# Layer 2's first seven products made from the un-normed residual, and normed as they leave

## The chip, the core and the metric

The kernel runs on one core of one Trainium2 chip. The metric is the device time of one execution in microseconds (us). Times are read from one profiled execution of the kernel before; the changed kernel is known here only as code and as the order of its instructions.

## What is computed

One inference step of a 2-layer decoder trunk for 320 tokens (256 of a prompt, 8 x 8 of samples), 2048 channels, float32. Cut to what matters here:

```python
def layer_norm(x, g, b):
    mu = jnp.mean(xf, -1, keepdims=True)
    var = jnp.mean(jnp.square(xf - mu), -1, keepdims=True)
    return (xf - mu) * lax.rsqrt(var + LN_EPS) * g + b
...
def mixer_layer(x, ...):
    h = x @ w_in
    ...
    y = merged @ w_out
    x_new = layer_norm(alpha * x + y, ln_g, ln_b)
...
    for l in range(DEPTH):
        xp, ... = mixer_layer(xp, ...)
        xs, ... = mixer_layer(xs, ...)
```

So layer 2's input projection `x @ w_in` needs layer 1's norm, which needs the whole residual `alpha * x + y` of a token.

## The kernel before

Activations lie transposed: 128 channels on the partitions, the 320 tokens in the row. A vector of 2048 channels is 16 tiles of 128x320, four to a buffer (`[128, 4, T]`, T = 320). Weights come in blocks of 128x128, eight to a chunk of 128x1024. Everything is held as a high and a low part in float32r (`hl`, `split_h`, `split_l`): ACT copies the high part, DVE (or POOL) subtracts it for the low part. A block then costs three matmuls into one PSUM tile: high weight x high tile, low x high, high x low (`block`, `block_low`).

`run` walks through a fixed list of jobs (`layer_groups`), a job being one 128-row strip of a product, with 16 blocks for most. Layer 2 begins with a group of four jobs that share each tile (kc 0, vc 0, qc 0, qc 1: attention's keys, values and queries), 16 x 12 products; then qc 2, qc 3, kc 1 and vc 1 alone, 48 products each. Eight blocks make a chunk: the first group is eight chunks, a single job two. Chunk c + 2's high split is issued at the start of chunk c, its low split in the middle; a low split goes to POOL when the kernel's own count of DVE's work is high. The PSUM tiles of such jobs are three (`pd`), and a job that ends is read out by its `done_` function.

All engines take their instructions in the order in which the program issues them (`manual_schedule`), so the order of the Python code sets the work. Background work (attention, retention) is stepped by `pump` once a chunk.

At the end of a layer `done_wo` adds each strip of the out-projection to the residual in `z` and sums it and its square over the tiles in `S` and `Q`. After strip 15, PE sums both over the partitions (`token_sums`, 6 small matmuls), DVE and ACT make mean and reciprocal deviation of each token, and PE spreads them over the partitions (`token_rows`, 2 x 3 matmuls). `norm` then centres (tiles 1 to 15 on POOL), scales (DVE), applies scale and offset and copies the high part (ACT) and subtracts for the low part (DVE). Its generator `rest` is written two to three tiles deep, and `need_x(k + 3)` steps it ahead of each tile of the first group:

```python
            for k in range(16):
                if k < 12:
                    center(k + 4, nc.gpsimd)
                if k < 13:
                    scaled(k + 3)
                if k < 14:
                    high(k + 2)
                if k:
                    low(k)
                yield
```

Lines of helpers in the profile: L196 is `mm`, L205 `tr`, L175 `act` (copies too), L182 `tt`, L186 `stt`, L191 `ts`.

Of the kernel before, what the change touches and what calls it, by code (L numbers as in the profile page):

```python
# [17 lines left out]
D = 2048  # L18
DEPTH = 2
NP = 256  # L20
NB, NT = 8, 8
T = NP + NB * NT
PAST = 1024
HA, DK, DV = 4, 128, 256
# [16 lines left out]
def att_rows(t):  # L41

    p, g = divmod(t, 4)
    lo, hi = (2 * p) * 4 + g, (2 * p + 1) * 4 + g
    return np.concatenate([np.arange(lo * 64, lo * 64 + 64), np.arange(hi * 64, hi * 64 + 64)])


# [43 lines left out]
class Job:  # L91
    __slots__ = ("kind", "i", "ps", "left", "w")

    def __init__(self, kind, i):
        self.kind, self.i, self.ps, self.left = kind, i, None, n_k(kind)


class Step:
# [200 lines left out]
    def setup(self):  # L299
        nc, io = self.nc, self.io  # L300
        self.ident = self.const("ident", [128, 128])
        make_identity(nc, self.ident[:])
        self.ident_r = self.cp.tile([128, 128], F32R, tag="ident_r", name="ident_r")
        nc.vector.tensor_copy(out=self.ident_r, in_=self.ident)
        self.ones = self.const("ones", [128, 128])
        nc.vector.memset(self.ones, 1.0)
        self.ones_r = self.cp.tile([128, 128], F32R, tag="ones_r", name="ones_r")
        nc.vector.memset(self.ones_r[:].bitcast(F32), 1.0)
        yield
# [15 lines left out]
        self.pscale = self.const("pscale", [128, DEPTH, 8], io["pool_scale"])  # L325
        self.lng = self.const("lng", [128, DEPTH, 16], io["ln_g"])
        self.lnb = self.const("lnb", [128, DEPTH, 16], io["ln_b"])
        self.bmask = self.const("bmask", [128, 4, 80], io["c_bmask"])
# [5 lines left out]
    def run(self):  # L334
# [30 lines left out]
        for layer in range(DEPTH):  # L365
            if layer:
                self.begin_layer(layer)
            for grp in layer_groups():
                jobs = [Job(kind, i) for kind, i in grp]
                self.before(jobs[0].kind, jobs[0].i)  # L370
                for k in range(n_k(grp[0][0])):
                    if len(jobs) > 1:
                        self.need_x(min(k + 3, 15))
                    for n, job in enumerate(jobs):
                        if pos == 0:
                            self.split_h(c + 2)
                        if pos == CH // 2:
                            self.split_l(c + 2)
                            self.load(c + 6)
                        self.block(job, k, c, pos)  # L380
                        pos += 1
# [11 lines left out]
    def block(self, job, k, c, pos):  # L393
        if job.ps is None:
            if job.kind == "qc" and job.i == 1:
                job.ps = self.p([128, T])
            else:
                job.ps = self.pd.tile([128, T], F32, tag="d", name="d")
# [14 lines left out]
    def part(self, pair, k):  # L413
        return pair[0][k // 4][:, k % 4, :], pair[1][k // 4][:, k % 4, :]

# [17 lines left out]
    def begin_layer(self, l):  # L433
        self.l, zs = l, getattr(self, "z", None)
        self.gated, self.pt, self.acc, self.sig = {}, {}, None, {}
        self.xk = 0
        self.x_gen = self.x_from_input() if l == 0 else self.norm(l - 1, zs, False)
        self.oC = [None, None]
# [5 lines left out]
    def need_x(self, k):  # L444
        while self.xk <= k:
# [4 lines left out]
            self.xk += 1  # L450

    def x_from_input(self):
        self.x = ([], [])
        for k in range(16):
            if k % 4 == 0:
                self.x[0].append(self.g([128, 4, T], F32R, name=f"xh{k}"))
                self.x[1].append(self.g([128, 4, T], F32R, name=f"xl{k}"))
            h, lo = self.part(self.x, k)
# [3 lines left out]
    def before(self, kind, i):  # L462
# [11 lines left out]
        if kind == "wo" and i == 0:  # L474
            self.z = [self.g([128, 4, T], name=f"z{n}") for n in range(4)]


# [243 lines left out]


    def done_kc(self, p, ps):
        nc, l = self.nc, self.l
        kv = self.g([128, 2, T], name="kv")
        self.copy(kv[:, 0, :], ps)
        nc.gpsimd.dma_start(out=self.io["o_wk"][l, p], in_=kv[:, 0, 128:T])
# [6 lines left out]
    def done_vc(self, p, ps):  # L734
        nc, l = self.nc, self.l
        kv = self.att[p]["kv"]
        self.copy(kv[:, 1, :], ps)
        nc.gpsimd.dma_start(out=self.io["o_wv"][l, p], in_=kv[:, 1, 128:T])
        self.att[p]["q"] = self.g([128, 4, T], name="qC")

    def done_qc(self, t, ps):
        p, g = divmod(t, 4)
        self.copy(self.att[p]["q"][:, g, :], ps)
        if g == 3:
# [241 lines left out]
    def done_wo(self, j, ps):  # L986
# [10 lines left out]
        if j == 1:  # L997
            self.drain("misc")
            for i in range(2):
                zi = self.z[0][:, i, :]  # L1000
                self.tt(zi, zi, self.cen, ALU.subtract)
            self.S = self.m([128, T], name="S")
            self.Q = self.m([128, T], name="Q")
# [4 lines left out]
        self.tt(self.S, self.S, z, ALU.add)  # L1008
        self.tt(self.Q, self.Q, sq, ALU.add)
        if j < 15:  # L1010
            n = self.z[(j + 1) // 4][:, (j + 1) % 4, :]
# [6 lines left out]
        if j == 15:  # L1018
            self.pS, self.pQ = self.token_sums(self.S), self.token_sums(self.Q)

    def center(self, z):
# [6 lines left out]

    def norm(self, l, zs, final):
        nc = self.nc  # L1030
        st = self.s(16)
        mu, ms, v, y, t = (st[:, 3 * i:3 * i + 3] for i in range(5))
        tile_of = lambda k: zs[k // 4][:, k % 4, :]
        M = self.m([128, T], name="M")

# [3 lines left out]
        def affine(k, out):  # L1039
            g, b = self.lng[:, l, k:k + 1], self.lnb[:, l, k:k + 1]  # L1040
            self.act(out=out, in_=tile_of(k), func=AF.Identity, bias=b, scale=g)

        def affine_v(k, out):
            self.ts(out, tile_of(k), self.lng[:, l, k:k + 1], self.lnb[:, l, k:k + 1])
# [5 lines left out]
        self.act(out=t, in_=v, func=AF.Sqrt)  # L1050
        pM = self.token_rows(mu)
        self.copy(M, pM)
        self.rsqrt(y, v, t)
        pR = self.token_rows(y)
        if final:
            return self.last(tile_of, center, affine, affine_v, pR)
        center(0)
        for k in range(1, 4):
            center(k, nc.gpsimd)
        self.x = ([], [])  # L1060
        for k in range(4):
            self.x[0].append(self.g([128, 4, T], F32R, name=f"xh{k}"))
            self.x[1].append(self.g([128, 4, T], F32R, name=f"xl{k}"))

        def scaled(k):
            self.tt(tile_of(k), tile_of(k), pR, ALU.mult)

        first = {}

        def high(k):  # L1070
            h = self.part(self.x, k)[0]
            if k < 2:
                affine(k, h)
                first[k] = self.m([128, T], name="x0")
                affine_v(k, first[k])
            else:
                affine(k, tile_of(k))
                self.copy(h, tile_of(k))

        def low(k):  # L1080
            h, lo = self.part(self.x, k)
            self.tt(lo, first.get(k, tile_of(k)), h.bitcast(F32), ALU.subtract)

        def rest():
            for k in range(2):
                scaled(k)
                high(k)
            low(0)
            scaled(2)
            for k in range(16):  # L1090
                if k < 12:
                    center(k + 4, nc.gpsimd)
                if k < 13:
                    scaled(k + 3)
                if k < 14:
                    high(k + 2)
                if k:
                    low(k)
                yield

        return rest()

    def last(self, tile_of, center, affine, affine_v, pR):
        nc = self.nc
        R = self.m([128, T], name="R")
# [36 lines left out]
    def finish(self):  # L1142
        self.norm(DEPTH - 1, self.z, True)

# [140 lines left out]
```

## Time and profile before

| | |
|---|---|
| median of 3 runs | 2310.35 us (2309.80 to 2310.91) |
| the profiled execution | 2310.74 us, of which the span is 2309.0 |
| busy share of PE, DVE, ACT, POOL | 98%, 53%, 41%, 8% |
| matmuls | 15660 records, a dense product of 320 columns every 0.147 us |
| granted TensorE clock over the span | 0.992 |

PE is TensorE's matmul, DVE VectorE, ACT ScalarE, POOL GpSimd, SP the engine that issues most DMAs. A group of rows gives busy time, then the mean of one instruction; an idle time stands before the group with what ended it. In a timeline the first number is the start in us from the start of the span, the second the time from the first start to the last end.

### The profile page before, as it was taken

The numbers are of one execution on the slowest core, as the hardware profiler recorded it, in microseconds if no ns is written. First come the engines' busy times: TensorE is split into PE (matmuls) and PEld (weight loads), VectorE is DVE, ScalarE is ACT, GpSimd is POOL, SyncE is SP. The second block draws the span as 40 slices with busy tenths as digits, with TensorE's granted clock in tenths as the row PEclk, the third lists the DMA queues.
The fourth block names the chain that finished last, engine by engine and source line by source line (L and its number), as shares of the span: only waits on it lengthen the run. The fifth ranks groups of instructions, "written<-read, shape, count | busy, mean of one in ns | idle before, by whom it ended". The sixth has DMA issues, their size and how long they took to land.

```text
span 2309.0 us, 37695 instructions
## 1 busy us (share of the span) xinstructions
PE 2273.1 (98%) x15660; PEld 2218.0 (96%) x15660; DVE 1222.3 (53%) x1826; ACT 945.8 (41%) x1536; POOL 182.9 (8%) x190
## 2 busy tenths in 40 slices
PE   8999999999999999999999999999999999999997
PEld 8997999999999999999998989999999999999997
DVE  4568465443444444446665775553434434444566
ACT  4544445333433343333365444443334333433333
POOL 1114000000000000000031230000000000000001
PEclk9999999999999999999999999999999999999998
DMA  7433455444444444444353344554444444444442
GB/s 274 137 137 131 163 189 179 155 151 146 147 154 150 152 146 153 149 151 151 129 196 119 131 136 153 194 183 150 152 148 154 146 149 143 157 154 146 146 150 98
DMA packets 97628, 354.91 MB, mean 154 GB/s; under 512 B 11521, under 2 KB 11969, under 8 KB 97393
## 3 DMA queue, kind: packets, MB, share of 16 engines
q1 hardware_dynamic: 93312, 335.87, 43.5%
q0 software_dynamic: 4144, 16.64, 2.0%
q8 instruction: 122, 2.00, 0.4%
q14 instruction: 50, 0.40, 0.1%
HBM read 338.51 MB, written 17.88 MB: 154 GB/s over the span
## 4 chain that ended last, share of the span: by engine, by line
PE 93%; DVE 5%; ACT 0%; DMA 0%; issue 0%; SPq 0%; DVEq 0%
PE d L196 87%; PE p L196 4%; DVE win L182 1%; PE p L205 1%; PE p L200 1%; DMA w<-w 0%; DVE sc L191 0%; DVE l L182 0%; DVE s L186 0%; DVE z L182 0%; DVE s L182 0%; DVE s L752 0%; DVE pp L186 0%; DVE sc L186 0%; DVE pp L182 0%
## 5 line engine op out<-in xcount | busy, mean ns | idle before, releaser
L196 PE MATMUL d<-xh,h 128*128 128x320 f32 x3424 | 1073.4, 314 | 15.6 <-ACT xh L175 6.9
L182 DVE TENSOR_TENSOR l<-w,h 128x1024 fp32r<-128x1024 f32 (+1 forms) x562 | 699.3, 1245 | 724.6 <-ACT h L175 723.7
L196 PE MATMUL d<-xh,l 128*128 128x320 f32 x3424 | 1060.5, 310 | 0.9 <-DVE l L182 0.9
L196 PE MATMUL d<-xl,h 128*128 128x320 f32 x3424 | 1050.2, 310 | 0.0
L175 ACT ACTIVATE h<-w 128x1024 fp32r<-128x1024 f32 (+1 forms) x597 | 627.5, 1052 | 495.1 <-PE d L196 363.1
L196 PEld LDWEIGHTS d<-xh,h 128*128 128x128 f32 x3424 | 645.3, 188 | 28.5 <-ACT xh L175 7.8
L196 PEld LDWEIGHTS d<-xh,l 128*128 128x128 f32 x3424 | 645.5, 189 | 2.1 <-DVE l L182 1.8
L196 PEld LDWEIGHTS d<-xl,h 128*128 128x128 f32 x3424 | 642.1, 188 | 0.0
L196 PE MATMUL d<-mgh,h 128*128 128x320 f32 x512 | 158.8, 310 | 0.0
L196 PE MATMUL d<-mgh,l 128*128 128x320 f32 x512 | 158.3, 309 | 0.0
L196 PE MATMUL d<-mgl,h 128*128 128x320 f32 x512 | 158.3, 309 | 0.0
L175 ACT ACTIVATE sig<-d 128x320 f32<-128x320 f32 x96 | 42.0, 437 | 226.0 <-PE d L196 226.0
L182 POOL TENSOR_TENSOR l<-w,h 128x1024 fp32r<-128x1024 f32 x35 | 84.9, 2432 | 226.6 <-ACT h L175 191.5
L196 PEld LDWEIGHTS d<-mgh,h 128*128 128x128 f32 x512 | 96.1, 188 | 0.2
L196 PEld LDWEIGHTS d<-mgh,l 128*128 128x128 f32 x512 | 96.1, 188 | 0.2
L196 PEld LDWEIGHTS d<-mgl,h 128*128 128x128 f32 x512 | 96.1, 188 | 0.0
L182 POOL TENSOR_TENSOR acc<-acc,ya 128x320 f32<-128x320 f32 x32 | 28.2, 880 | 822.2 <-DVE ya L182 822.2
L196 PE MATMUL d<-gch,l 128*128 128x320 f32 x256 | 79.2, 309 | 0.0
L196 PE MATMUL d<-gah,h 128*128 128x320 f32 x256 | 79.2, 309 | 0.0
L196 PE MATMUL d<-gal,h 128*128 128x320 f32 x256 | 79.2, 309 | 0.0
L196 PE MATMUL d<-gbh,h 128*128 128x320 f32 x256 | 79.2, 309 | 0.0
L196 PE MATMUL d<-gcl,h 128*128 128x320 f32 x256 | 79.2, 309 | 0.0
(234 smaller groups left out, 2119.3 us busy)
## 6 DMA issues: line engine op xcount, KB each, us to landing
w<-w SPq DMA_DIRECT2D x595, 512.0 KB, 3.3
s<-s SPq DMA_DIRECT2D x16, 512.0 KB, 5.6
o_rets<-s POOLq DMA_DIRECT2D x16, 512.0 KB, 5.1
bias<-bias_p SPq DMA_DIRECT2D x8, 512.0 KB, 5.5
o_x<-z SPq DMA_DIRECT2D x8, 320.0 KB, 2.2
ck<-ck SPq DMA_DIRECT2D x4, 512.0 KB, 4.7
cv<-cv SPq DMA_DIRECT2D x4, 512.0 KB, 6.1
xin<-x SPq DMA_DIRECT2D x3, 640.0 KB, 11.8
```

The lines of the kernel that those rows point to most:

```text
L175: self.nc.scalar.activation(out=out, in_=in_, func=func, **kw)
L182: (eng or self.nc.vector).tensor_tensor(out=out, in0=a, in1=b, op=op)
L196: self.nc.tensor.matmul(out, lhsT=lhsT, rhs=rhs, start=start, stop=stop)
L200: self.nc.tensor.matmul(out, lhsT=lhsT, rhs=rhs, start=False, stop=True, skip_group_check=True)
L205: self.nc.tensor.transpose(out, in_, ident[:n, :n])
```

## The change

The first seven jobs of layer 2 (`EARLY`: kc 0, vc 0, qc 0 to 3, kc 1) no longer take the normed tiles. `unnormed` writes the residual times the norm's scale over layer 1's dead input tiles, as each strip of the out-projection is done; two columns more (T to TU = 322) hold scale and offset themselves. A product of these has the sums over the channels of (z x scale x weight), of (scale x weight) and of (offset x weight), and `take` norms it on the way out: with M and R, the tokens' mean and reciprocal deviation in rows, it computes (product - M x column 0) x R + column 1. The sums, M and R are made by a generator that is stepped among the first group's tiles; behind that it norms the 16 tiles, for the other jobs and the residual, one tile a step. `drain_x` has them all normed ahead of the first job that needs them (vc 1). One const tile less holds identity and ones each, and scale and offset come in one load.

```diff
+EARLY = {("kc", 0), ("vc", 0), ("qc", 0), ("qc", 1), ("qc", 2), ("qc", 3), ("kc", 1)}
...
-                    if len(jobs) > 1:
-                        self.need_x(min(k + 3, 15))
+                    if layer == 0:
+                        if len(jobs) > 1:
+                            self.need_x(min(k + 3, 15))
+                    elif not jobs[0].early:
+                        self.drain_x()
+                    elif len(jobs) > 1 or k % 4 == 3:
+                        next(self.x_gen, None)
...
+        if job.early:
+            return tuple(t[k // 4][:, k % 4, :] for t in self.u)
...
+    def take(self, out, ps):
+        if ps.shape[1] == T:
+            self.copy(out, ps)
+            return
+        w = self.s(2)
+        t = self.m([128, T], name="tk")
+        self.copy(w, ps[:, T:])
+        self.stt(t, self.M, w[:, 0:1], ps[:, 0:T], ALU.mult, ALU.subtract)
+        self.tt(t, t, self.R, ALU.mult)
+        self.act(out=out, in_=t, func=AF.Identity, bias=w[:, 1:2], scale=-1.0)
...
+    def unnormed(self, k):
+        if self.l < DEPTH - 1:
+            h, lo = self.part(self.x, k)
+            z, g = self.z[k // 4][:, k % 4, :], self.lngb[:, self.l, k, 0:1]
+            self.act(out=h, in_=z, func=AF.Copy, scale=g)
+            self.stt(lo, z, g, h.bitcast(F32), ALU.mult, ALU.subtract)
...
+    def norm(self, l, zs):
+        tile_of = lambda k: zs[k // 4][:, k % 4, :]
+        yield
+        yield
+        self.pS, self.pQ = self.token_sums(self.S), self.token_sums(self.Q)
+        mu, v, y, t = self.stats()
+        self.rsqrt(y, v, t)
+        yield
+        yield
+        self.M = self.m([128, T], name="M")
+        self.copy(self.M, self.token_rows(mu))
+        yield
+        self.R = self.m([128, T], name="R")
+        self.copy(self.R, self.token_rows(y))
+        yield
+        self.x = ([], [])
+        for k in range(16):
...
+            self.tt(z, z, self.M, ALU.subtract)
+            self.tt(z, z, self.R, ALU.mult)
+            self.act(out=z, in_=z, func=AF.Identity, bias=self.lngb[:, l, k, 1:2], scale=self.lngb[:, l, k, 0:1])
+            self.hl(h, lo, z)
+            yield
```

The order of the instructions moves on PE, DVE, ACT and POOL; on SP it stays. On PE, before, at the end of layer 1's out-projection (mgh and mgl are the merged branches, d and p PSUM tiles, h and l the weights' two parts):

```order
L196 MATMUL d<-mgl_8782,h 128x320
L196 MATMUL p<-ones,S 128x1 x3
L196 MATMUL p<-ones,Q 128x1 x3
L196 MATMUL p<-ident,s 128x128 x2
L196 MATMUL p<-ident,s 128x64
L196 MATMUL p<-ident,s 128x128 x2
L196 MATMUL p<-ident,s 128x64
L196 MATMUL d<-xh_11371,h 128x320
```

And now, behind the second tile of layer 2's first group:

```order
L202 MATMUL d<-xh_110,h 128x322
L202 MATMUL d<-xh_110,l 128x322
L202 MATMUL p<-xh_110,h 128x322
L202 MATMUL p<-xh_110,l 128x322
L202 MATMUL d<-xl_111,h 128x322 x3
L202 MATMUL p<-xl_111,h 128x322
L202 MATMUL p<-ones_r,S 128x1 x3
L202 MATMUL p<-ones_r,Q 128x1 x3
L202 MATMUL d<-xh_110,h 128x322
```

The sums went behind 24 products of layer 2, and the two sets of rows behind 48 and 60. On DVE, before, in the middle of the norm (xl is a low part, z the residual, the p behind z the broadcast reciprocal deviation):

```order
L182 TENSOR_TENSOR z_10242<-z_10242,p 128x320
L182 TENSOR_TENSOR xl_11374<-z_10242,xh_11373 128x320
L182 TENSOR_TENSOR l<-w,h 128x1024
L182 TENSOR_TENSOR z_10243<-z_10243,p 128x320
L182 TENSOR_TENSOR xl_11374<-z_10242,xh_11373 128x320
L182 TENSOR_TENSOR z_10243<-z_10243,p 128x320
```

And now, where the norm begins:

```order
L188 TENSOR_TENSOR l<-w,h 128x1024 x2
L188 TENSOR_TENSOR z_10237<-z_10237,M 128x320
L188 TENSOR_TENSOR z_10237<-z_10237,R 128x320
L188 TENSOR_TENSOR xl_11500<-z_10237,xh_11499 128x320
L188 TENSOR_TENSOR z_10237<-z_10237,M 128x320
L188 TENSOR_TENSOR z_10237<-z_10237,R 128x320
L188 TENSOR_TENSOR xl_11500<-z_10237,xh_11499 128x320
```

A tile's three instructions stand together, and the next tile's follow; the centring came over from POOL, where its 15 rows are gone and seven low splits stand in this stretch in the place of three. Two low splits remain among the 16 tiles on DVE. On ACT, before, at the end of the first group:

```order
L175 ACTIVATE z_10244<-z_10244,lnb,lng 128x320
L175 ACTIVATE xh_11377<-z_10244 128x320
L175 ACTIVATE h<-w 128x1024 x3
L175 ACTIVATE kv<-d 128x320 x2
L175 ACTIVATE qC<-d 128x320
L175 ACTIVATE qC<-p 128x320
```

And now (tk is the product on its way through `take`, s the two columns):

```order
L181 ACTIVATE xh_11663<-z_10239 128x320
L181 ACTIVATE s<-d 128x2
L181 ACTIVATE kv<-tk,s 128x320
L181 ACTIVATE s<-d 128x2
L181 ACTIVATE kv<-tk,s 128x320
L181 ACTIVATE s<-d 128x2
L181 ACTIVATE qC<-tk,s 128x320
L181 ACTIVATE s<-p 128x2
L181 ACTIVATE qC<-tk,s 128x320
L181 ACTIVATE h<-w 128x1024
```

The read-outs were four copies in a row; now two of DVE's instructions stand between each pair of ACT's, behind ten tiles of the norm.

## Rows read from the trace of the kernel before

**Rows 1.** The page: span; busy us, share of the span, instructions of each engine.

```profile
span 2309.0 us, 37695 instructions
PE 2273.1 (98%) x15660; PEld 2218.0 (96%) x15660; DVE 1222.3 (53%) x1826; ACT 945.8 (41%) x1536; POOL 182.9 (8%) x190
```

**Rows 2.** The page: the chain that ended last, by engine.

```profile
PE 93%; DVE 5%; ACT 0%; DMA 0%; issue 0%; SPq 0%; DVEq 0%
```

**Rows 3.** Busy us of each engine by stretch around the layer boundary.

```profile
core 0: us, PE busy (x) PEld busy (x) DVE busy (x) ACT busy (x) POOL busy (x), PEclk, DMA share, GB/s
1144.40:1151.40 7.00, 4.55 (x25) 4.28 (x24) 4.45 (x15) 1.76 (x4) 2.10 (x3) 0.66 0.31 101
1151.40:1157.00 5.60, 5.59 (x21) 5.59 (x22) 5.56 (x11) 3.98 (x8) 5.60 (x7) 0.51 0.00 0
1157.00:1163.00 6.00, 6.00 (x43) 6.00 (x42) 5.45 (x9) 5.88 (x11) 6.00 (x5) 1.00 0.27 90
1163.00:1181.50 18.50, 18.50 (x128) 18.50 (x127) 17.75 (x19) 12.98 (x20) 10.40 (x6) 1.00 0.49 167
1181.50:1200.00 18.50, 18.41 (x126) 18.15 (x125) 6.13 (x5) 7.26 (x11) 2.03 (x6) 1.00 0.73 248
```

**Rows 4.** PE in order of time, across the boundary and where the clock rises.

```profile
1144.11 0.31 PE L196 MATMUL d<-mgl,h 128*128 128x320 f32 x1
1145.61 0.80 PE L196 MATMUL p<-ones,S 128*128 128x1 f32 x6 [1.20 <-DVE S L182]
1146.28 1.04 PE L196 MATMUL p<-ones,Q 128*128 128x1 f32 x6
1147.18 2.97 PE L196 MATMUL p<-ident,s 128*128 128x128 f32 x12
1151.41 0.63 PE L196 MATMUL d<-xh,h 128*128 128x320 f32 x1 [1.27 <-ACT xh L175]
...
1155.84 0.47 PE L196 MATMUL d<-xh,h 128*128 128x320 f32 x1
1156.11 0.47 PE L196 MATMUL d<-xh,l 128*128 128x320 f32 x1
...
1157.52 0.30 PE L196 MATMUL d<-xh,h 128*128 128x320 f32 x1
1157.66 0.31 PE L196 MATMUL d<-xh,l 128*128 128x320 f32 x1
```

**Rows 5.** PE in order of time: attention's first transposes in layer 2.

```profile
1200.13 0.60 PE L205 MATMUL p<-ident,kv 128*128 128x128 f32 x4
```

**Rows 6.** DVE's groups, 1000 to 1144 us: busy us, mean ns, idle before.

```profile
L182 DVE TENSOR_TENSOR l<-w,h 128x1024 fp32r<-128x1024 f32 x41 | 50.0, 1223 | 29.4 <-ACT h L175 29.2
L182 DVE TENSOR_TENSOR S<-S,z 128x320 f32<-128x320 f32 x14 | 6.9, 492 | 0.5
L186 DVE SCALAR_TENSOR_TENSOR z<-xl,cen 128x320 f32<-128x320 f32 x14 | 6.8, 484 | 0.0
```

**Rows 7.** ACT's groups: two of 1136 to 1150 us, three of 1150 to 1180.

```profile
L175 ACT ACTIVATE M<-p 128x320 f32<-128x320 f32 x1 | 0.4, 437 | 1.0 <-PE p L196 1.0
L175 ACT ACTIVATE s<-s 128x3 f32<-128x3 f32 x1 | 0.2, 204 | 2.1 <-DVE s L186 2.1
...
L175 ACT ACTIVATE z<-z,lnb,lng 128x320 f32<-128x320 f32 x14 | 9.0, 642 | 1.3 <-DVE z L182 1.3
L175 ACT ACTIVATE h<-w 128x1024 fp32r<-128x1024 f32 x8 | 8.4, 1048 | 3.7 <-PE p L196 3.7
L175 ACT ACTIVATE xh<-z 128x320 fp32r<-128x320 f32 x14 | 6.6, 472 | 0.4
```

**Rows 8.** DVE's subtractions in order of time, with and without a POOL split beside.

```profile
1170.49 0.47 DVE L182 TENSOR_TENSOR xl<-z,xh 128x320 fp32r<-128x320 f32 x1
1171.30 2.58 DVE L182 TENSOR_TENSOR xl<-z,xh 128x320 fp32r<-128x320 f32 x1
1176.84 2.69 DVE L182 TENSOR_TENSOR xl<-z,xh 128x320 fp32r<-128x320 f32 x1
...
1171.11 2.42 POOL L182 TENSOR_TENSOR l<-w,h 128x1024 fp32r<-128x1024 f32 x1 [5.16 <-ACT h L175]
```

**Rows 9.** Stretches around a later PE gap, columns as in rows 3.

```profile
1342.00:1345.60 3.60, 0.27 (x2) 0.00 (x0) 3.43 (x8) 0.41 (x2) 1.73 (x2) 0.87 0.67 221
1345.60:1351.40 5.80, 5.79 (x37) 4.86 (x37) 5.59 (x12) 4.06 (x14) 2.87 (x2) 0.50 0.27 109
1351.40:1356.00 4.60, 4.60 (x33) 4.59 (x34) 4.43 (x15) 2.53 (x8) 2.07 (x2) 0.99 0.39 118
```

More of the change, by code (lines that the diff above doesn't have):

```diff
@@ L22 @@
 T = NP + NB * NT
+TU = T + 2
 PAST = 1024
@@ L91, with __init__ @@
 class Job:
-    __slots__ = ("kind", "i", "ps", "left", "w")
-    def __init__(self, kind, i):
+    __slots__ = ("kind", "i", "ps", "left", "w", "early")
+    def __init__(self, kind, i, layer):
         self.kind, self.i, self.ps, self.left = kind, i, None, n_k(kind)
+        self.early = layer > 0 and (kind, i) in EARLY
 class Step:
@@ L300, in setup @@
         nc, io = self.nc, self.io
-        self.ident = self.const("ident", [128, 128])
-        make_identity(nc, self.ident[:])
         self.ident_r = self.cp.tile([128, 128], F32R, tag="ident_r", name="ident_r")
-        nc.vector.tensor_copy(out=self.ident_r, in_=self.ident)
-        self.ones = self.const("ones", [128, 128])
+        self.ident = self.ident_r[:].bitcast(F32)
+        ident = self.m([128, 128], name="ident0")
+        make_identity(nc, ident[:])
+        nc.vector.tensor_copy(out=self.ident_r, in_=ident)
+        self.ones_r = self.cp.tile([128, 128], F32R, tag="ones_r", name="ones_r")
+        self.ones = self.ones_r[:].bitcast(F32)
         nc.vector.memset(self.ones, 1.0)
-        self.ones_r = self.cp.tile([128, 128], F32R, tag="ones_r", name="ones_r")
-        nc.vector.memset(self.ones_r[:].bitcast(F32), 1.0)
         yield
@@ L325, in setup @@
         self.pscale = self.const("pscale", [128, DEPTH, 8], io["pool_scale"])
-        self.lng = self.const("lng", [128, DEPTH, 16], io["ln_g"])
-        self.lnb = self.const("lnb", [128, DEPTH, 16], io["ln_b"])
+        self.lngb = self.const("lngb", [128, DEPTH, 16, 2], io["ln_gb"])
         self.bmask = self.const("bmask", [128, 4, 80], io["c_bmask"])
@@ L368, in run @@
             for grp in layer_groups():
-                jobs = [Job(kind, i) for kind, i in grp]
+                jobs = [Job(kind, i, layer) for kind, i in grp]
                 self.before(jobs[0].kind, jobs[0].i)
                 for k in range(n_k(grp[0][0])):
-                    if len(jobs) > 1:
-                        self.need_x(min(k + 3, 15))
+                    if layer == 0:
[5 more added lines that the diff above has]
+                        next(self.x_gen, None)
                     for n, job in enumerate(jobs):
@@ L394, in block @@
         if job.ps is None:
+            n = TU if job.early else T
             if job.kind == "qc" and job.i == 1:
-                job.ps = self.p([128, T])
+                job.ps = self.p([128, n])
             else:
-                job.ps = self.pd.tile([128, T], F32, tag="d", name="d")
+                job.ps = self.pd.tile([128, n], F32, tag="d", name="d")
         job.w = h, lo = self.H[c][:, pos, :], self.L[c][:, pos, :]
@@ L413, in part @@
     def part(self, pair, k):
-        return pair[0][k // 4][:, k % 4, :], pair[1][k // 4][:, k % 4, :]
+        return pair[0][k // 4][:, k % 4, 0:T], pair[1][k // 4][:, k % 4, 0:T]
     def pair(self, n, name):
@@ L436, in begin_layer @@
         self.xk = 0
-        self.x_gen = self.x_from_input() if l == 0 else self.norm(l - 1, zs, False)
+        if l:
+            self.u = self.x
+        self.x_gen = self.x_from_input() if l == 0 else self.norm(l - 1, zs)
         self.oC = [None, None]
@@ L450, in need_x, with drain_x @@
             self.xk += 1
+    def drain_x(self):
+        for _ in self.x_gen:
+            pass
     def x_from_input(self):
@@ L455, in x_from_input @@
             if k % 4 == 0:
-                self.x[0].append(self.g([128, 4, T], F32R, name=f"xh{k}"))
-                self.x[1].append(self.g([128, 4, T], F32R, name=f"xl{k}"))
+                self.x[0].append(self.g([128, 4, TU], F32R, name=f"xh{k}"))
+                self.x[1].append(self.g([128, 4, TU], F32R, name=f"xl{k}"))
             h, lo = self.part(self.x, k)
@@ L475, in before @@
             self.z = [self.g([128, 4, T], name=f"z{n}") for n in range(4)]
+            if self.l < DEPTH - 1:
+                for n in range(4):
+                    self.hl(
+                        self.x[0][n][:, :, T:], self.x[1][n][:, :, T:], self.lngb[:, self.l, 4 * n:4 * n + 4, :]
+                    )
     def rotary(self, ps, dst, scale):
@@ L725, in done_kc @@
         kv = self.g([128, 2, T], name="kv")
-        self.copy(kv[:, 0, :], ps)
+        self.take(kv[:, 0, :], ps)
         nc.gpsimd.dma_start(out=self.io["o_wk"][l, p], in_=kv[:, 0, 128:T])
@@ L736, in done_vc @@
         kv = self.att[p]["kv"]
-        self.copy(kv[:, 1, :], ps)
+        self.take(kv[:, 1, :], ps)
         nc.gpsimd.dma_start(out=self.io["o_wv"][l, p], in_=kv[:, 1, 128:T])
@@ L742, in done_qc @@
         p, g = divmod(t, 4)
-        self.copy(self.att[p]["q"][:, g, :], ps)
+        self.take(self.att[p]["q"][:, g, :], ps)
         if g == 3:
@@ L1001, in done_wo @@
                 self.tt(zi, zi, self.cen, ALU.subtract)
+                self.unnormed(i)
             self.S = self.m([128, T], name="S")
@@ L1009, in done_wo @@
         self.tt(self.Q, self.Q, sq, ALU.add)
+        if j > 1:
+            self.unnormed(j)
         if j < 15:
@@ L1017, in done_wo @@
             self.act(out=dummy, in_=self.ones[:, 0:1], func=AF.Sqrt)
-        if j == 15:
+        if j == 15 and self.l == DEPTH - 1:
             self.pS, self.pQ = self.token_sums(self.S), self.token_sums(self.Q)
+    def unnormed(self, k):
+        if self.l < DEPTH - 1:
+            h, lo = self.part(self.x, k)
+            z, g = self.z[k // 4][:, k % 4, :], self.lngb[:, self.l, k, 0:1]
+            self.act(out=h, in_=z, func=AF.Copy, scale=g)
+            self.stt(lo, z, g, h.bitcast(F32), ALU.mult, ALU.subtract)
     def center(self, z):
@@ L1027, in center, with stats @@
         yield
-    def norm(self, l, zs, final):
-        nc = self.nc
+    def stats(self):
         st = self.s(16)
         mu, ms, v, y, t = (st[:, 3 * i:3 * i + 3] for i in range(5))
-        tile_of = lambda k: zs[k // 4][:, k % 4, :]
-        M = self.m([128, T], name="M")
-        def center(k, eng=None):
-            self.tt(tile_of(k), tile_of(k), M if eng else pM, ALU.subtract, eng)
[L1039 to L1044, printed above, removed]
         self.ts(mu, self.pS, 1.0 / D)
@@ L1050, in norm, with last, center, affine @@
         self.act(out=t, in_=v, func=AF.Sqrt)
+        return mu, v, y, t
+    def norm(self, l, zs):
[15 more added lines that the diff above has]
+        for k in range(16):
+            if k % 4 == 0:
+                self.x[0].append(self.g([128, 4, T], F32R, name=f"xh{k}"))
+                self.x[1].append(self.g([128, 4, T], F32R, name=f"xl{k}"))
+            z = tile_of(k)
+            h, lo = self.part(self.x, k)
+            self.tt(z, z, self.M, ALU.subtract)
[3 more added lines that the diff above has]
+            yield
+    def last(self):
+        nc, l = self.nc, DEPTH - 1
+        tile_of = lambda k: self.z[k // 4][:, k % 4, :]
+        M = self.m([128, T], name="M")
+        def center(k, eng=None):
+            self.tt(tile_of(k), tile_of(k), M if eng else pM, ALU.subtract, eng)
+        def affine(k, out):
+            g, b = self.lngb[:, l, k, 0:1], self.lngb[:, l, k, 1:2]
+            self.act(out=out, in_=tile_of(k), func=AF.Identity, bias=b, scale=g)
+        def affine_v(k, out):
+            self.ts(out, tile_of(k), self.lngb[:, l, k, 0:1], self.lngb[:, l, k, 1:2])
+        mu, v, y, t = self.stats()
         pM = self.token_rows(mu)
@@ L1054, in norm @@
         pR = self.token_rows(y)
[L1055 to L1104, printed above, removed]
         R = self.m([128, T], name="R")
@@ L1142, in finish @@
     def finish(self):
-        self.norm(DEPTH - 1, self.z, True)
+        self.last()
 def constants():
@@ L1249 @@
         pool_scale=perkt(a["pool_scale"], 8),
-        ln_g=perkt(a["ln_g"], 16),
-        ln_b=perkt(a["ln_b"], 16),
+        ln_gb=np.stack([perkt(a["ln_g"], 16), perkt(a["ln_b"], 16)], axis=3),
         **bias_tables(a["rel_bias"]),
```

## The prediction, before the changed kernel had run

> **What bounds the kernel now.** The page's busy shares come first: PE is busy 98% of the span, DVE 53%, ACT 41% [rows 1], and the chain that ended last lies on PE for 93% [rows 2]. So time is lost or won only where PE waits, or where its clock is down. The stretches around the layer boundary show one such place [rows 3]: from 1144.4 to 1151.4 us PE has almost nothing to do, and from 1151.4 to 1157.0 it runs at a granted clock of 0.51, its lower level of 1.2 GHz. In order of time [rows 4]: layer 1's last product starts at 1144.11, then come the token sums and the broadcast rows, and layer 2's first product starts at 1151.41, waiting for the first normed tile. Its products then follow each other at 0.267 us until 1157 and at 0.147 us behind it [rows 4]. The boundary thus costs 7.3 us of gap and, for 24 products, 24 x (0.267 - 0.147) = 2.9 us of slow clock. That is what the change aims at. One more thing is to be seen [rows 3]: while the norm runs, DVE is busy 17.75 of 18.5 us between 1163.0 and 1181.5 and 6.13 of 18.5 behind it. DVE, not PE, is the engine without slack there.
>
> **The change part by part.** I count from t = 0 at 1144.11, up to one landmark: the product behind the first half of kc1, the seventh product. 312 products stand ahead of it (192 in the first group, 48 each in qc 2 and 3, 24 in kc1). Before, attention's first transposes stand there, at 1200.13 [rows 5], so t = 56.0; by hand 312 x 0.147 + 7.3 + 2.9 = 56.1.
>
> *PE alone.* The seven products need only tiles 0 to 15 of the un-normed residual, which are written one by one during the out-projection. Each such job lasts 48 x 0.147 = 7.0 us and now holds on DVE two splits of 1.22 and six operations of about 0.49 [rows 6], 5.4 us: covered, cost zero (without that cover, 0.5 us a job). The eight tiny splits of scale and offset are hidden in the same way; so is the setup, one memset and one load fewer. The gap and the slow clock go. The 12 small products (sums, two broadcast rows) move in among the others; at the lower clock and with waits they took 4.5 us [rows 4], I take 3. Two more columns in 336 products are at most 336 x 0.147 x 2/320 = 0.3 us. The landmark would come at 45.9 + 3 = 48.9: 7.1 us earlier.
>
> *DVE and ACT.* The norm of the 16 tiles, which was written out two tiles deep, with its centring on POOL, becomes one serial row for each tile: DVE centres and scales, ACT applies scale and offset and copies, DVE subtracts. DVE takes its instructions in order, and the next tile's centring stands behind this tile's subtraction (order rows of DVE), so nothing overlaps inside it: 0.49 + 0.49 + 0.64 + 0.47 + 0.47 = 2.56 us a tile [rows 6 to 8]. PE's pace is 12 x 0.147 = 1.76 us for a tile in the first group. What stands in that queue until the last tile is normed:
> - The start: the second broadcast row goes ahead of tile 5's products, 5 x 1.76 + 3 = 11.8, and its copy takes 0.44 [rows 7]: 12.2.
> - 16 tiles x 2.56 = 41.0.
> - Two weight splits left on DVE in that time, 2 x 1.22 = 2.4 [rows 6].
> - Six of the seven weight splits that go to POOL. A POOL split takes 2.42 us, and a DVE subtraction that met one took 2.58 and 2.69 instead of 0.47 [rows 8]: DVE stood until POOL was done. So each costs DVE between 0 (it falls where DVE waits for ACT anyway, 1.11 us a tile) and 2.4. It starts when ACT's half of the split is done, about when DVE's scaling ends, so the 1.11 us cover part of it: I take 2.42 - 1.11 = 1.3, in all 7.8 (0 to 14.5).
> - Four read-outs in a row, those of the first group. Each is now ACT (0.20), two DVE operations (0.48 + 0.49) and ACT again (0.64) [rows 6, 7], and the next one's first ACT step stands behind the last step of this one: 4 x 1.8 = 7.2. That of qc 2 adds its DVE part, 1.0.
>
> Sum: 12.2 + 41.0 + 2.4 + 7.8 + 7.2 + 1.0 = 71.6. The seventh POOL split belongs to the chunk behind the landmark; it follows ACT's half (1.05), which starts during the last subtraction, and takes 2.42 [rows 7, 8]: about 3.1 more. PE can pass the landmark at t = 74.7, not at 48.9.
>
> PE will not wait there in one piece. It is fed by weight splits that stand behind the norm in DVE's queue and are issued two chunks ahead, so it first starves late in the first group. Then qc 2 needs a PSUM tile that kc 0's read-out frees, behind ten tiles' norm: I expect the longest wait there, 7 to 10 us. Some more of 2 to 3 us follow.
>
> *The clock after such waits.* A PE gap of 3.3 us in the trace (1342.3 to 1345.6) was followed by 5.8 us at a granted clock of 0.50 [rows 9]. So the clock will fall again, but while PE waits for DVE a slow product costs nothing; I take 0. The Trainium skill (TensorE: Matmul & The Clock Gate, section "A second HAM failure mode: psum-queue depth-cycling") says that many short idles between groups of matmuls make the clock go back and forth and cost throughput. By it the sum would be some 4.6 us higher; that is the first rival.
>
> Behind the landmark nothing moves: the order of SP is the same, that of PE too. The change is 74.7 - 56.0 = +18.7 us. The profiled execution took 2310.74 us (span 2309.0), 0.4 over the median of 2310.35: **2310.7 + 18.7 = 2329.4 us**.
>
> **Rivals.**
> - *The clock stays low.* From t = 45 to 75 PE has some 120 products to do; at 0.267 us these are 32 us instead of the 30 that DVE leaves, and the first 5.8 us behind lose 2.6 more: 4.6 us, 2334 us. For it speaks that one gap of 3.3 us was enough [rows 9]; against it, that the clock came back under a dense row of products each time [rows 3, 9].
> - *POOL's splits fall into DVE's waits.* Then they hold nothing: 7.8 us less, 2321.6 us. The rows with 2.6 us speak against it [rows 8]. The Trainium skill (SBUF — State Buffer, "Who interferes with whom") has it that a VectorE instruction with two SBUF inputs stands still for a whole GpSimd instruction that reads SBUF, if that began first; the trace agrees, with 2.58 and 2.69 us against 0.47.
> - *Faster: DVE and ACT keep ahead of PE.* Then the gap and the slow clock go and only the 3 us come back: 7.1 less, 2303.6 us. All but the tiles is 71.6 + 3.1 - 41.0 = 33.7 us, so this needs 48.9 - 33.7 = 15.2 us for 16 tiles, 0.95 us a tile. The two engines would have to overlap tiles as they do before, where one tile's scaling stood between another's copy and its subtraction; the queue no longer allows it, and DVE alone has 1.45 us a tile.
> - *No change*: at (56.0 - 33.7)/16 = 1.39 us a tile gain and loss cancel, 2310.7 us. The same speaks against it.
>
> **How the numbers follow.** The forecast, 2329.4, has 0.72; the low clock 0.10; the free POOL splits 0.10; faster 0.05; no change 0.03. A measurement can tell about 0.2%, 4.6 us, from no change. So slower has 0.72 + 0.10 + 0.10 = 0.92, same 0.03, faster 0.05. The range reaches down past the free splits to 2318, for start and read-outs that overlap a little more, and up to 2339: the low clock, or splits that hold DVE 2.4 us each (+6.7), with some 3 us for what neither covers. It leaves out the two other cases, 0.08, and some 0.1 at its ends.
>
> **What would show it.** No PE gap of 7 us at 1144, sums and rows among the products of 128x322, no slow clock there. Then waits of PE for DVE and POOL, together some 26 us, between 25 and 75 us behind the boundary, the longest at the start of qc 2's product. On DVE, centring to next centring about 2.6 us, with idle time that ACT ends; POOL splits beside DVE subtractions of over 1 us. The last tile normed some 71 us after the boundary, and the transposes of attention about 19 us later than before. It is wrong if the tiles follow each other at under 1.5 us, if PE passes into kc1 without a wait over 2 us, or if the time is lost elsewhere, as in layer 1, where the slices of x now lie 1288 bytes apart instead of 1280: no row shows that pitch, and I take it at zero.

## The result, and the profile after

The changed kernel takes **2333.89 us** (median of 4 runs, 2332.83 to 2334.88) against 2310.12 (4 runs): a ratio of 1.0101 [1.0086, 1.0116], slower by 23.8 us. The forecast was 2329.4 with a range of 2318 to 2339, and the time lies inside it. The profiled execution took 2333.99 us, 23.25 over that of before.

The page of the kernel after: span, busy us of each engine, and the chain that ended last (they answer to [rows 1] and [rows 2]).

```profile
span 2332.2 us, 37762 instructions
PE 2280.2 (98%) x15660; PEld 2223.9 (95%) x15660; DVE 1237.3 (53%) x1868; ACT 957.9 (41%) x1566; POOL 175.8 (8%) x178
...
PE 91%; DVE 7%; ACT 2%; issue 0%; DMA 0%; POOL 0%; SPq 0%; ACTq 0%; DVEq 0%
```

PE is busy 7.1 us longer, and the span is 23.2 longer: most of the loss is waiting, and not all of it. The chain gives two more points to DVE and two to ACT. PE's timeline of the kernel after tells where; these are its rows with a wait, the small products, and the two landmarks (they answer to [rows 4] and [rows 5]).

```profile
1150.98 0.31 PE L202 MATMUL d<-mgl,h 128*128 128x320 f32 x1
1154.93 0.72 PE L202 MATMUL p<-ones_r,S 128*128 128x1 f32 x6
1155.52 0.81 PE L202 MATMUL p<-ones_r,Q 128*128 128x1 f32 x6
1159.82 0.78 PE L202 MATMUL p<-ident_r,s 128*128 128x128 f32 x6
1162.27 0.78 PE L202 MATMUL p<-ident_r,s 128*128 128x128 f32 x6
1182.44 0.63 PE L202 MATMUL d<-xh,l 128*128 128x322 f32 x1 [2.94 <-DVE l L188]
1195.18 0.64 PE L202 MATMUL d<-xh,h 128*128 128x322 f32 x1 [7.59 <-DVE tk L192]
1205.26 0.41 PE L202 MATMUL d<-xh,l 128*128 128x322 f32 x1 [0.64 <-POOL l L188]
1211.38 0.41 PE L202 MATMUL d<-xh,l 128*128 128x322 f32 x1 [2.29 <-POOL l L188]
1216.96 0.41 PE L202 MATMUL d<-xh,h 128*128 128x322 f32 x1 [1.91 <-ACT h L181]
1219.39 0.41 PE L202 MATMUL d<-xh,l 128*128 128x322 f32 x1 [2.01 <-POOL l L188]
1224.43 0.60 PE L211 MATMUL p<-ident_r,kv 128*128 128x128 f32 x4
```

The loss falls into three parts. Layer 1's last product starts at 1150.98 instead of 1144.11: **+6.9 us, lost before the boundary is reached**. From there to attention's transposes it is 1224.43 - 1150.98 = 73.45 us instead of 56.02: **+17.4**. Behind that, 0.8 us come back up to the last product, mostly behind the later gap of [rows 9], where the clock stays at 0.50 for 3.4 us and not for 6.8. The sum, 23.5, is the difference of the profiles to 0.3 us.

Busy time of each engine in five stretches behind the boundary of the kernel after (they answer to [rows 3]).

```profile
1150.90:1163.00 12.10, 12.10 (x88) 11.84 (x87) 6.70 (x15) 4.41 (x7) 0.00 (x0) 1.00 0.50 167
1163.00:1179.50 16.50, 16.45 (x110) 15.95 (x109) 10.09 (x19) 8.93 (x14) 2.68 (x1) 1.00 0.28 95
1179.50:1195.20 15.70, 5.17 (x25) 4.90 (x24) 9.42 (x17) 7.57 (x13) 5.29 (x2) 0.81 0.21 68
1195.20:1209.00 13.80, 13.16 (x73) 12.74 (x73) 8.37 (x15) 6.47 (x13) 3.84 (x4) 0.85 0.48 166
1209.00:1225.40 16.40, 10.10 (x54) 9.27 (x54) 10.29 (x15) 6.96 (x13) 7.25 (x4) 0.90 0.20 65
```

No engine is full in the third and the last of them: PE is busy 5.17 us of 15.70 and 10.10 of 16.40, DVE 9.42 and 10.29, ACT 7.57 and 6.96. Before, DVE was busy 17.75 of 18.5 us while the norm ran [rows 3]. This is a row of instructions that wait for each other. DVE's timeline of the kernel after shows it: the norm's first tiles, a later one, two of `take`'s read-outs, the last subtraction and the read-out behind it.

```profile
1163.20 0.49 DVE L188 TENSOR_TENSOR z<-z,M 128x320 f32<-128x320 f32 x1
...
1165.50 0.49 DVE L188 TENSOR_TENSOR xl<-z,xh 128x320 fp32r<-128x320 f32 x1 [1.23 <-ACT xh L181]
1165.91 0.49 DVE L188 TENSOR_TENSOR z<-z,M 128x320 f32<-128x320 f32 x1
1166.43 0.49 DVE L188 TENSOR_TENSOR z<-z,R 128x320 f32<-128x320 f32 x1
1168.15 0.49 DVE L188 TENSOR_TENSOR xl<-z,xh 128x320 fp32r<-128x320 f32 x1 [1.23 <-ACT xh L181]
...
1174.58 1.38 DVE L188 TENSOR_TENSOR xl<-z,xh 128x320 fp32r<-128x320 f32 x1 [1.23 <-ACT xh L181]
...
1196.40 0.55 DVE L192 SCALAR_TENSOR_TENSOR tk<-M,s,d 128x320 f32<-128x320 f32 x1 [0.75 <-ACT s L181]
1196.98 0.49 DVE L188 TENSOR_TENSOR tk<-tk,R 128x320 f32<-128x320 f32 x1
1198.22 0.55 DVE L192 SCALAR_TENSOR_TENSOR tk<-M,s,d 128x320 f32<-128x320 f32 x1 [0.75 <-ACT s L181]
...
1221.83 0.49 DVE L188 TENSOR_TENSOR xl<-z,xh 128x320 fp32r<-128x320 f32 x1 [1.22 <-ACT xh L181]
1222.84 0.55 DVE L192 SCALAR_TENSOR_TENSOR tk<-M,s,d 128x320 f32<-128x320 f32 x1 [0.52 <-ACT s L181]
1223.42 2.14 DVE L188 TENSOR_TENSOR tk<-tk,R 128x320 f32<-128x320 f32 x1
```

From one subtraction to the next it is 2.65 us, of which DVE stands 1.23 for ACT. At 1174.58 the subtraction takes 1.38 instead of 0.49: it ends at 1175.96, 0.35 us behind the first of POOL's seven splits here, as POOL's timeline shows (the first and the last of them).

```profile
1172.93 2.68 POOL L188 TENSOR_TENSOR l<-w,h 128x1024 fp32r<-128x1024 f32 x1 [360.53 <-ACT h L181]
...
1222.83 2.39 POOL L188 TENSOR_TENSOR l<-w,h 128x1024 fp32r<-128x1024 f32 x1 [3.49 <-ACT s L181]
```

### The profile page after: what moved, and what is told of

It reads as the page before. It is cut to its first block, busy times and chain, and to the rows that moved or that the text cites. A ratio compares the mean times of both kernels' runs of the same rounds, so it can differ in the third digit from the quotient of the medians.

```text
span 2332.2 us, 37762 instructions
## 1 busy us (share of the span) xinstructions
PE 2280.2 (98%) x15660; PEld 2223.9 (95%) x15660; DVE 1237.3 (53%) x1868; ACT 957.9 (41%) x1566; POOL 175.8 (8%) x178
## 4 chain that ended last, share of the span: by engine, by line
PE 91%; DVE 7%; ACT 2%; issue 0%; DMA 0%; POOL 0%; SPq 0%; ACTq 0%; DVEq 0%
PE d L202 85%; PE p L202 4%; DVE win L188 1%; PE p L211 1%; DVE z L188 1%; PE p L206 1%; DVE l L188 1%; DVE xl L188 1%; ACT z L181 1%; DVE sc L197 0%; DVE s L192 0%; DMA w<-w 0%; ACT xh L181 0%; DVE s L188 0%; ACT h L181 0%
## 5 line engine op out<-in xcount | busy, mean ns | idle before, releaser
L202 PE MATMUL d<-xh,h 128*128 128x320 f32 (+1 forms) x3424 | 1076.8, 315 | 25.1 <-DVE tk L192 7.6
L202 PE MATMUL d<-xh,l 128*128 128x320 f32 (+1 forms) x3424 | 1062.2, 310 | 8.5 <-POOL l L188 4.9
L202 PE MATMUL d<-xl,h 128*128 128x320 f32 (+1 forms) x3424 | 1052.8, 311 | 0.0
L188 POOL TENSOR_TENSOR l<-w,h 128x1024 fp32r<-128x1024 f32 x39 | 95.0, 2441 | 611.9 <-ACT h L181 580.8
L202 PE MATMUL d<-gbh,l 128*128 128x320 f32 x256 | 79.1, 309 | 0.0
L202 PE MATMUL d<-gch,h 128*128 128x320 f32 x256 | 79.1, 309 | 0.0
```

The costliest lines, as they stand in the source:

```text
L188: (eng or self.nc.vector).tensor_tensor(out=out, in0=a, in1=b, op=op)
L202: self.nc.tensor.matmul(out, lhsT=lhsT, rhs=rhs, start=start, stop=stop)
```

## The experiments

Two questions were open: what lost 6.9 us in layer 1, where the change was to cost nothing, and whether the +17.4 behind it is the serial norm, the POOL splits or the products' own 322 columns.

### Layer 1: the place of x's slices

The first kernel is the one before with x's four slices 1288 bytes apart, as the change has them in layer 1, and nothing else of it but the single const tiles that make room. The second, its control, has the same const tiles and the same room, taken by another buffer.

```diff
# pitch_in_before
...
-                self.x[0].append(self.g([128, 4, T], F32R, name=f"xh{k}"))
+                self.x[0].append(self.g([128, 4, T + 2], F32R, name=f"xh{k}"))
...
-        return pair[0][k // 4][:, k % 4, :], pair[1][k // 4][:, k % 4, :]
+        return pair[0][k // 4][:, k % 4, 0:T], pair[1][k // 4][:, k % 4, 0:T]
# slot_in_before
...
-        a1 = self.g([128, 1280], name="a1")
+        a1 = self.g([128, 1288], name="a1")
```

> The kernel before, with one identity and one set of ones as in the change, and layer 1's x tiles laid out with 322 columns a slice (1288 bytes) of which 320 are used; no early products. If the pitch is what makes layer 1 longer (products at 147.8 ns instead of 146.7): layer 1's last product moves from 1144.1 to about 1149.5, the time by +5.4 to about 2315.5. If layer 1's loss has to do with the rest of the change: 2310.1, layer 1 ends at 1144.

> The kernel before, with one identity and one set of ones as in the change, and one other buffer of the large pool widened by 8 elements, so that all of the pool's buffers lie 5152 bytes apart instead of 5120; x keeps slices of 1280 bytes. If the pitch of the slices counts: 2310.1 to 2310.5, products at 146.7 ns. If the buffers' own addresses count: about 2315.5, as with the pitch.

Measured: 2315.27 us against 2309.96 for the pitch, a ratio of 1.0025 [1.0016, 1.0035], so +5.3 us; 2309.97 for the room alone, 1.0000 [0.9991, 1.0010]. The same two rows of PE's timeline, the product behind the gap at 200 us and the first of the out-projection, show it. Before:

```profile
202.90 0.42 PE L196 MATMUL d<-xh,h 128*128 128x320 f32 x1 [3.34 <-DVE rt L182]
...
1031.08 0.31 PE L196 MATMUL d<-mgh,h 128*128 128x320 f32 x1
```

After:

```profile
204.40 0.41 PE L202 MATMUL d<-xh,h 128*128 128x320 f32 x1 [3.34 <-DVE rt L188]
...
1037.26 0.31 PE L202 MATMUL d<-mgh,h 128*128 128x320 f32 x1
```

The kernel before with the pitch:

```profile
204.51 0.41 PE L196 MATMUL d<-xh,h 128*128 128x320 f32 x1 [3.34 <-DVE rt L182]
...
1037.37 0.31 PE L196 MATMUL d<-mgh,h 128*128 128x320 f32 x1
```

The stretch lasts 828.18, 832.86 and 832.86 us: the pitch alone gives the whole 4.7. Taken over each job's 48 products of x (66 to 68 jobs), their starts lie 146.7 ns apart before and 147.8 in both others, and 146.8 in `slot_in_before`; in layer 2, whose x has the old pitch in all of them, 146.7 to 146.9. With 4176 such products in the stretch, 1.1 ns each are 4.6 us.

Is it the pitch, or that three slices of four then start 8, 16 and 24 bytes past a multiple of 64? In the next kernel all start 8 bytes past one, at the old pitch.

```diff
# start_8_bytes
...
-                self.x[0].append(self.g([128, 4, T], F32R, name=f"xh{k}"))
+                self.x[0].append(self.g([128, 1288], F32R, name=f"xh{k}")[:, 2:2 + 4 * T].rearrange("p (k t) -> p k t", t=T))
...
```

> As slot_in_before, but layer 1's x slices start 8 bytes into their buffers, at a pitch of 1280 bytes. If it is where a slice starts that slows a product: all 16 slices are now off, products in layer 1 at 147.8 ns or more, 2315 to 2317. If it is the pitch as such: 2310.

Measured: 2318.57 us, a ratio of 1.0035 [1.0021, 1.0049], +7.9; starts 148.4 ns apart. So it is where a slice starts. With all slices off it costs more than with three of four. The trace of `pitch_in_before` shows the same inside each buffer: the products of its first slice, whose start is the old one, lie 146.9 ns apart, those of its fourth, 24 bytes off, 148.6; before and in `slot_in_before` both have 146.6 to 146.9.

The other way round: the change, with the un-normed residual in tiles of its own, x back at its old pitch, and the tiny splits of scale and offset spread among the strips of the out-projection.

```diff
# own_tiles
-        if l:
-            self.u = self.x
...
-                self.x[0].append(self.g([128, 4, TU], F32R, name=f"xh{k}"))
+                self.x[0].append(self.g([128, 4, T], F32R, name=f"xh{k}"))
...
-            h, lo = self.part(self.x, k)
+            if k % 4 == 0:
+                for n in range(2):
+                    self.u[n].append(self.g([128, 4, TU], F32R, name=f"u{'hl'[n]}{k}"))
+                self.hl(self.u[0][-1][:, :, T:], self.u[1][-1][:, :, T:], self.lngb[:, self.l, k:k + 4, :])
+            h, lo = self.part(self.u, k)
```

> The change with the un-normed tiles and their two columns in eight buffers of their own; layer 1's x keeps slices of 1280 bytes, and the tiny splits of scale and offset stand among the strips of the out-projection instead of together ahead of it. The norm stays serial. If layer 1's loss is the pitch (5.4 us) and the eight tiny splits ahead of the out-projection (0.5 us): layer 1's last product at 1144 to 1145 instead of 1151, time 2328. If the early products' 322 columns cost in layer 1 in another way: 2334.

Measured: 2329.57 us against 2310.69, a ratio of 1.0083 [1.0069, 1.0097]. The stretch above is 828.21 us again, and layer 1's last product starts at 1145.18, 1.1 us behind that of before. Some 0.4 us of it is there at the kernel's start already. Another 0.6 us is a second thing that the prediction had at zero: where the out-projection's first two strips are both written un-normed, a weight split comes late. The kernel after has the same wait:

```profile
1059.56 0.42 PE L202 MATMUL d<-mgh,l 128*128 128x320 f32 x1 [0.31 <-DVE l L188]
```

From the start of the product ahead of it, at 1058.94, it is 0.62 us where others take 0.15.

### The boundary: the norm's row

The next kernel leaves out the norm of the 16 tiles: all of layer 2's products read the un-normed tiles, so its output is another. It keeps sums, rows and read-outs. With less work on DVE, the kernel's own count also gives POOL no weight split in this stretch, so norm and POOL splits are left out together here; `splits_on_dve` below takes the splits alone.

```diff
# no_norm
-        self.x = ([], [])
-        for k in range(16):
...
-            self.hl(h, lo, z)
-            yield
+        self.x = self.u
```

> The change without the norm of the 16 tiles: layer 2's other products and its residual take the un-normed tiles, so its output is another; sums, rows, the seven products and their read-outs stay. If the serial norm on DVE and ACT is what PE waits for: nearly all of the 20 us of waits between 1179 and 1220 go, some 22 us less, about 2311.5, which is the time of before plus layer 1's loss less the boundary's gain. If the low clock or the read-outs alone make the loss: less than 10 us are won, 2324 or more.

Measured: 2316.16 us, a ratio of 1.0029 [1.0018, 1.0041], some 4.7 us above what was expected. PE's rows with a wait, and the landmark:

```profile
1182.09 0.41 PE L202 MATMUL d<-xh,h 128*128 128x322 f32 x1 [0.40 <-DVE tk L192]
1189.66 0.41 PE L202 MATMUL d<-xh,h 128*128 128x322 f32 x1 [0.22 <-ACT h L181]
1190.92 0.41 PE L202 MATMUL d<-xh,l 128*128 128x322 f32 x1 [0.85 <-DVE l L188]
...
1201.56 0.60 PE L211 MATMUL p<-ident_r,kv 128*128 128x128 f32 x4
```

The waits of 17.4 us are down to 1.5, and the landmark stands 51.5 us behind layer 1's last product (at 1150.03), 4.5 earlier than before and 21.9 earlier than after. So the read-outs and the 322 columns are not the loss; the norm's row is, with the splits that come with it. Most of what the expectation missed lies behind the landmark, where layer 2's x now has the 1288-byte pitch too: products 147.8 ns apart there as well, and 3.5 us more than before up to the last one.

Now the same work in another order: the next tile's centring and scaling go ahead of this tile's subtraction.

```diff
# two_deep
-            self.hl(h, lo, z)
...
+        scaled(0)
+        for k in range(16):
+            high(k)
+            if k < 15:
+                scaled(k + 1)
+            low(k)
             yield
```

> The change with the same operations of the norm in another order: a tile's centring and scaling stand ahead of the subtraction of the tile before it, so that DVE has work while ACT applies scale and offset. If DVE's and ACT's taking turns is the cause: about 1.9 us a tile with its share of splits instead of 2.6 and more, some 10 us less, about 2324. If the sum of DVE's work or POOL's splits is the cause, and not the order: 2333.9 within 3 us.

Measured: 2324.95 us, a ratio of 1.0069 [1.0054, 1.0084]: 9 us better than the change, by order alone. The landmark comes at t = 65.2. That it is not more lies in part with POOL, as DVE's timeline of this kernel shows:

```profile
1169.50 2.58 DVE L188 TENSOR_TENSOR z<-z,R 128x320 f32<-128x320 f32 x1
1172.01 0.48 DVE L188 TENSOR_TENSOR xl<-z,xh 128x320 fp32r<-128x320 f32 x1
...
1173.33 0.48 DVE L188 TENSOR_TENSOR xl<-z,xh 128x320 fp32r<-128x320 f32 x1
1174.66 0.48 DVE L188 TENSOR_TENSOR xl<-z,xh 128x320 fp32r<-128x320 f32 x1
```

Undisturbed, a tile takes 1.33 us. But where the idle 1.23 us are gone, a POOL split holds DVE longer: 2.1 us in the first of these rows, and 1.3 to 2.2 in six of the seven, where it was 0.85 to 1.25. These six come to 10.8 us instead of 5.9. What else keeps it from more was not tried by itself.

Next, the change with the stretch's POOL splits given to DVE.

```diff
# splits_on_dve
-            if c > 8 and self.busy["v"] > 0.5 and self.busy["p"] < 0:
+            if c > 8 and not 0 <= c - NCHUNK // 2 < 16 and self.busy["v"] > 0.5 and self.busy["p"] < 0:
```

> The change with no weight split on POOL in layer 2's first 16 chunks; DVE does them all. If each POOL split holds DVE about as long as DVE's own split takes (1.0 to 1.3 us against 1.22): 2330 to 2335. If POOL's splits fall into DVE's waits for ACT and cost nothing: seven more splits of 1.22 us on DVE, 2339 or more.

Measured: 2332.23 us, a ratio of 1.0095 [1.0080, 1.0111], whose interval overlaps that of the change. All seven splits are on DVE now; the first of them, and the instruction behind it:

```profile
1174.70 1.22 DVE L188 TENSOR_TENSOR l<-w,h 128x1024 fp32r<-128x1024 f32 x1
1175.83 0.48 DVE L188 TENSOR_TENSOR z<-z,M 128x320 f32<-128x320 f32 x1
```

A split costs DVE's queue about the same by either engine: 1.13 us from the start of its own split to the next instruction's, against 0.85 to 1.25 of hold. One thing more moves with this edit: by the kernel's count of DVE's work, attention's first transposes come 96 products later, so the landmark can't be compared. The 314th product of x behind the boundary, ahead of which only those transposes differ on PE (some 0.35 us), can: it starts 74.05 us behind layer 1's last product here, and 74.29 in the change.

### All of it together

The last kernel takes the change and answers each finding: tiles of its own for the un-normed residual, the norm two tiles deep with the centring on POOL four tiles ahead, the scaling by the broadcast row in PSUM, `take`'s two columns copied by DVE, no weight splits on POOL in this stretch.

```diff
# combined, against own_tiles
-        self.copy(w, ps[:, T:])
+        self.nc.vector.tensor_copy(out=w, in_=ps[:, T:])
...
+            self.tt(z, z, pR, ALU.mult)
...
+                self.tt(tile_of(k), tile_of(k), self.M, ALU.subtract, self.nc.gpsimd)
...
         for k in range(16):
+            center(k + 4)
+            if k < 14:
+                scaled(k + 2)
+            if k < 15:
+                high(k + 1)
+            low(k)
```

> The early products with everything mended: un-normed tiles in buffers of their own, the norm two tiles deep with its centring on POOL and its scaling read from PSUM, the read-outs' two columns copied by DVE instead of ACT, no weight split on POOL in this stretch. If the two causes found so far are all of the loss: PE waits under 2 us in this stretch, the boundary's gain of some 5 to 7 us is left, 2304 to 2306, faster than both. If DVE has too much to do in any order: 2310 or more.

Measured: **2307.14 us** (11 runs) against 2310.69, a ratio of 0.9986 [0.9977, 0.9995]: a little faster than before, a little less than was expected, and 26.8 us faster than the change. PE's rows with a wait between the boundary and the landmark:

```profile
1179.55 0.39 PE L202 MATMUL d<-uh,h 128*128 128x322 f32 x1 [1.64 <-DVE tk L192]
1187.52 0.42 PE L202 MATMUL d<-uh,l 128*128 128x322 f32 x1 [0.51 <-DVE l L188]
1195.35 0.41 PE L202 MATMUL d<-uh,l 128*128 128x322 f32 x1 [0.48 <-DVE l L188]
1198.85 0.60 PE L211 MATMUL p<-ident_r,kv 128*128 128x128 f32 x4
```

Layer 1's last product starts at 1146.29, so the landmark is at t = 52.6 instead of 56.0: half of the 7.1 us that PE alone could win. 2.6 us of the other half are these waits. POOL still holds DVE here, by the centring: while that runs, to 1173.7, a subtraction takes 0.77 to 1.14 us instead of 0.48, and a weight split on DVE 1.9 instead of 1.22.

## Why the prediction was right, and the step that was wrong

**What held.** The boundary part was put at +18.7 and measured +17.4, with its cause: `no_norm` takes 21.9 us away, and `two_deep` 9 us without removing an operation. Term by term:

| | put at | measured |
|---|---|---|
| 12 small products | 3 us | 0.72 + 0.81 + 0.78 + 0.78 = 3.1 |
| start, to the first centring | 12.2 | 1163.20 - 1150.98 = 12.2 |
| a tile | 2.56 | 2.65 |
| hold by a POOL split | 1.3 (0 to 2.4) | 0.85 to 1.25 (1.33 to 1.74 instead of 0.49) |
| a read-out in the row of four | 1.8 | 1.82 (1196.40 to 1198.22) |
| last tile normed | t = 71.6 | 1222.3, t = 71.3 |
| the seventh POOL split's end | t = 74.7 | 1222.83 + 2.39 = 1225.22, t = 74.2 |
| the landmark | t = 74.7 | t = 73.45 |

The prediction set the landmark equal to the end of the seventh POOL split. The transposes and one product behind them don't need that split, so PE passes the landmark before it; the first product that does need it starts at 1225.27. The longest wait stood where it was put, at qc 2's first product, with 7.59 us (7 to 10). PE's waits were 17.4 us in sum and not some 26. The landmark is 24.5 us later than PE's own pace (48.9) would have it; some 5 of these are slow products, about 40 at 0.267 us instead of 0.147, which the prediction had put down as free and so should have taken out of the waits. The windows of the first two slow stretches show it (14 and 16 products, PE without a gap), and that around the third, of which 3.4 us are slow. About 1 us more goes to the products ahead of the six waits: they end 0.30 to 0.41 us after their start, and the next would have started after 0.147.

```profile
1182.50:1186.00 3.50, 3.50 (x14) 3.50 (x15) 2.17 (x5) 2.08 (x4) 0.47 (x1) 0.53 0.49 149
1195.20:1199.40 4.20, 4.20 (x16) 4.20 (x17) 2.53 (x5) 1.25 (x5) 1.15 (x2) 0.50 0.89 299
1219.40:1224.40 5.00, 5.00 (x23) 5.00 (x24) 3.19 (x6) 2.13 (x4) 1.57 (x1) 0.66 0.33 108
```

**The clock.** It fell as forecast: four stretches at 0.50, of 3.4, 6.8 and 3.4 us in the boundary part (from 1182.36, 1192.60 and 1219.90) and one later. Behind the first two PE next waited for DVE or POOL anyway. The last is the plainest: PE runs slowly from 1219.90 on, yet its next row that needs a POOL split starts 0.05 us after that split's end (1222.83 + 2.39).

```profile
1225.27 0.41 PE L202 MATMUL d<-xh,l 128*128 128x322 f32 x1
```

So the slow clock set no end there, and the rival in which it adds 4.6 us falls, although its 2334 us is almost the time measured: the number came from layer 1.

**The POOL splits** hold DVE, so the rival in which they are free falls: 1.33 to 1.74 us for the subtraction six times, and 2.14 for a product of `take` as in [rows 8]. The Trainium skill (SBUF — State Buffer, "Who interferes with whom") adds that a VectorE instruction with no more than one SBUF tensor among its inputs, outside the modes in which VectorE uses both its ports, isn't held. The traces agree: at 1222.84 `take`'s first step, with the PSUM tile as one of its two tiles, takes its usual 0.55 us beside a split begun at 1222.83, and its second, with two SBUF tiles, takes 2.14; in `combined` the scaling from PSUM keeps its 0.48 us beside POOL's centring, and the subtraction doesn't.

**Faster** was put down as needing 0.95 us a tile, which "the queue no longer allows". That is what the order of the change decides, not the idea: `combined` wins 3.5 us with a queue that allows it.

**What was wrong.** One step: "in layer 1, where the slices of x now lie 1288 bytes apart instead of 1280: no row shows that pitch, and I take it at zero". It measured +5.3 us by itself (`pitch_in_before`). The smaller one beside it, the un-normed work and the tiny splits "covered, cost zero", measured 0.6 us: averaged over a job the DVE work is covered, but the first two strips are written in a row. Together they are 5.9 of the 6.9 us lost ahead of the boundary. Another 0.6 was there at 26 us already, at the kernel's start, and is not the change's: `no_norm`, `two_deep` and `splits_on_dve`, which have its code up to the boundary, stand at -0.3, 0.1 and 0.3 us there. The clock differs in these executions: before, it is at its upper level from 13.5 us on; in the kernel after it was at 0.50 from 15.0 to 18.4 us. The total is 4.5 us too low: 6.9 of layer 1, less the 1.3 by which the boundary was put too high and the 0.8 that came back behind it, and 0.3 behind the last product. That it lies in the range nevertheless is in part luck: the room above the forecast was made for a clock that stays low and for longer holds, and neither of them filled it.

## What to carry to other kernels

Work that moves off the bottleneck's path must be costed in the queue that it moves to, instruction by instruction: here 16 tiles in series cost 2.65 us each, and 1.33 with the next tile's first steps ahead of this tile's last. When a tile gets a few columns more, look at where every slice of it starts, and for all its readers: two columns used by 336 products slowed the 5184 of layer 1 that read the same buffers. And an engine that is waiting hides a contention (0.85 to 1.25 us of a POOL split's hold), which grows (to 1.3 to 2.2) when the wait is optimised away.

## What was not expected of the hardware

The spacing of TensorE's products depends on where the moving slice starts in its row: 146.7 ns for 128x320 in float32r with every slice at a multiple of 64 bytes from the tile's start, 147.8 with starts at 0, 8, 16 and 24 past one, 148.4 with all at 8. Between these, the weights, their loads and the order are the same. That the buffers themselves are put elsewhere does nothing (`slot_in_before`, 1.0000). If the pool lays its buffers out 5152 bytes apart there, as was expected, every second one starts 32 bytes past a multiple of 64 as counted from the first, and that was free; the trace has no addresses to show it. Why the spacing depends on the start, and which other starts are free, wasn't tried.
